# Final norm written in place, merge additions on GpSimd, and another slot for one table at the half change of an eight-core decoder kernel

## The chip, the cores and the metric

The kernel runs on the 8 cores of one Trainium2 chip, each core with its own sequence. The metric is the device time of the slowest core in microseconds (us). Before the change it was 3667.8 us, the median of 3 runs (3666.34 to 3668.78).

## The reference, cut to what matters

```python
for l in range(4):                       # per layer; 2048 positions, width 1024
    h = rmsnorm(x, norm1_g)
    zb, zc, zv, zu, ga, gs = split(h @ w_in)
    ya = zb * conv_causal(zc * zv)                 # short convolution branch
    ys = s5(zu)                                    # diagonal state space branch
    gy = gelu(ys); ys = gy * sigmoid(gy @ w_glu + b_glu)
    m  = sigmoid(ga) * (ya @ wb_conv) + sigmoid(gs) * (ys @ wb_ssm)   # merge
    x  = x + m @ w_out
    x  = x + (silu(gate) * up) @ w_down            # gate, up = rmsnorm(x) @ w_gate_up
return rmsnorm(x, final_g), ...                    # final norm, then states
```

## The kernel before

A core computes its sequence in two halves of 1024 positions: 4 layers of half 0, final norm and store, 4 layers of half 1, final norm and store. The **half change** is the passage from the end of half 0 into layer 0 of half 1. Half 0 has column blocks of 384, 384 and 272, half 1 has two of 512. The program records operations with their tiles, and then a list scheduler *inside the program* fixes each engine's order for good, with its own estimate of durations and of one DMA bus. So order is decided by a model and waits by the chip.

```python
def dma(self, eng, fn, r, w, nbytes, prio=None, extra=0.0):   # S.dma
    o.dur = 0.9 if eng == "pool" else 0.06     # the model's cost of an issue
    o.nbytes = nbytes; o.extra = extra
# ... in schedule():
    beg = max(bus, t + dur + 0.6)
    bus = beg + o.nbytes / self.DBW            # the model's one bus
    o.end = bus + 1.3 + o.extra

SP_ = Pool("sc", NSC - 4, lambda s: SC[:, s, :], reserve=2)    # five SC slots
TABP = Pool("tab", 2, ...)                                     # two table slots
TABC = Pool("tabc", 1, lambda s: R[:, 8:16, :]...)             # one more in R

def norm(half, blk, l, which, src=None):
    # ... squares on ACT, sum by ones-matmuls on PE, Ln and Exp on ACT into rs
    for kt in range(8):
        if which == "fg":                      # the final norm
            o = SP_.new()
            dve(scalar_tensor_tensor(out=o, in0=xi(), scalar=g, in1=rs, mult, mult))
            S.dma("sp", dma_start(out=yT[half, :, kt, ...], in_=o[:, 0:npr]), ...)
            if 8 in blk.ss:
                S.dma("sp", dma_start(out=ysT[:, kt, :], in_=o[:, npr:npr + NS]), ...)

def layer(half, l, after_blk, before_fd2=None):
    for f0 in range(2):                        # the state space input zu
        for mt in range(2):
            # PE: zu = w_in part of H; ACT: R[:, YS + f] = zu
            S.dma("sp", dma_start(out=du[f], in_=R[:, YS + f]))    # to DRAM ...
            S.dma("sp", dma_start(out=ut_, in_=du[f]))             # ... and back: UU
    def ssm_f(f):                              # one quarter of the state space branch
        alias = [("R", t, s) for t in range(8, 16) for s in range(9)] if f == 2 else []
        tab = (TABC if f == 2 else TABP).new()
        S.dma("sp", dma_start(out=tab[:, 0:TW], in_=stash[l, f]))  # its table
        # PE: state matmuls ps<-UU,TAB; DVE/ACT: scan, RBT, VT; PE: ps<-VT,TAB; ACT: gelu
        S.dma("sp", dma_start(out=dy[f], in_=yt))                  # to DRAM ...
        S.dma("sp", dma_start(out=R[:, YS + f], in_=dy[f]))        # ... and back
    # convolution: PE zc, zv, zb; ACT SC, DVE CIN; then GLU on R; then the merge:
                    dve(tensor_tensor(out=sg, in0=sg, in1=po, op=mult))
                    dve(tensor_tensor(out=R[:, MT[j]], in0=t_, in1=sg, op=add))

def unstage(where):     # half 1's x was loaded into idle tiles; ACT copies it into X
    for blk in BLKS[1]:
        for k in range(8):
            act(activation(out=X[:, k, ...], in_=t[...], func=AF.Copy))
```

(Arguments are shortened. A TensorE matmul of 128 x 128 by 128 x 512 is named by the tiles: `ps<-H,RING` multiplies the normed activation H by a weight slot, `ps<-R,RING` multiplies R.)

## Time and profile before

| | before |
|---|---|
| median of 3 runs, us | 3667.8 |
| profiled run: slowest core 1, us | 3684.6 |
| spans of its cores, us | 3655.5 to 3684.6 |
| PE busy | 3527.6 us, 96% |

The page's first part (busy us, share of the span, instructions of each engine) and the first group of its fifth part (busy time, mean ns of one, idle time just before and what ended it), kernel before:

```profile
PE 3527.6 (96%) x23912; PEld 1987.8 (54%) x23912; DVE 1699.6 (46%) x3049; ACT 1134.0 (31%) x2144; POOL 439.7 (12%) x639
...
L667 PE MATMUL ps<-H,RING 128*128 128x512 bf16 (+2 forms) x12160 | 2216.8, 343 | 22.5 <-DVE H L722 9.1
```

TensorE is the bound, and what this change can win is its pauses. Where it runs freely it is at its rate: one piece of the chain that ended last is 1008 matmuls of 512 columns in 217.60 us, 215.9 ns each. That agrees with the 215.7 ns that the Trainium skill gives for a warm N = 512 ("TensorE: Matmul & The Clock Gate", section "Wait — 56ns, not 53.3ns?").

The table by stretches around the half change, kernel before. Columns: stretch, its length, busy us (and instructions) of five engines, granted clock, DMA share, GB/s:

```profile
1896.00:1925.00 29.00, 25.02 (x149) 15.20 (x147) 23.41 (x43) 13.86 (x31) 2.11 (x4) 0.88 0.29 62
1925.00:2005.00 80.00, 59.41 (x653) 30.91 (x652) 38.54 (x71) 35.23 (x73) 3.17 (x6) 0.87 0.94 229
2005.00:2120.00 115.00, 114.85 (x533) 51.94 (x532) 54.65 (x82) 36.50 (x61) 7.91 (x15) 1.00 0.49 95
```

The first busy figure is PE: 3.98 + 20.59 us idle in the first two stretches. The waits of PE from 1890 to 2060 us (us in total, times, longest):

```profile
PE ps L1028 <- ACT X L1306: 10.0, 1, 10.0
PE ps L667 <- ACT CIN L1173: 5.6, 1, 5.6
PE ps L667 <- DVE X L1240: 4.0, 1, 4.0
PE ps L1102 <- DVE VT L1065: 2.9, 1, 2.9
```

They add up to 22.5 us. And the wait of DVE in the same passage that the change aims at:

```profile
DVE SC L712 <- DMA yT<-SC: 28.1, 8, 13.5
```

The final norm's writes need one of five SC slots, and a slot is free only when its store has landed. Timeline of SyncE's DMA issues (start, us, then what; the row's length runs from the first of its issues to the end of the last), kernel before:

```profile
1926.44 0.38 SPq L987 DMA_DIRECT2D du<-R  x1
...
1929.84 11.77 SPq L987 DMA_DIRECT2D du<-R  x3
1942.72 7.25 SPq L716 DMA_DIRECT2D yT<-SC  x4
1950.12 0.38 SPq L990 DMA_DIRECT2D UU<-du  x1
```

The first UU load leaves at 1950.12 us. Timeline of PE, with the idle time before a row and its releaser in brackets:

```profile
1923.67 20.88 PE L667 MATMUL ps<-H,RING 128*128 128x512 bf16 x96
1954.51 1.07 PE L1028 MATMUL ps<-UU,TAB 128*64 128x64 bf16 x32 [9.96 <-ACT X L1306]
...
1962.82 5.30 PE L667 MATMUL ps<-H,RING 128*128 128x512 bf16 x16 [5.65 <-ACT CIN L1173]
```

PE does 96 matmuls, stands for 10 us, and starts the first state matmul (`ps<-UU,TAB`) at 1954.51 us; the 16 after the next pause take 331 ns each (5.30 / 16) instead of 216. The DMA issues of 1896 to 2005 us (KB of one, median us from issue to landing):

```profile
yT<-SC SPq DMA_DIRECT2D x16, 192.0 KB, 4.2
...
du<-R SPq DMA_DIRECT2D x4, 256.0 KB, 18.3
```

### The profile page before, as it was taken

Reading aid. Unit: us, or ns where it says so; the run is one execution under the profiler, and the core shown is the slowest. Engines: PE = TensorE matmul, PEld = TensorE weight load, DVE = VectorE, ACT = ScalarE, POOL = GpSimd, SP = SyncE. Lnnn points to the kernel's source line nnn. Section 1 sums busy time; section 2 is a strip of 40 time slices with the busy share of each in tenths; the row PEclk is TensorE's granted clock in tenths of the full one; section 3 lists DMA queues with packets and bytes.
Section 4 is the critical chain, followed back from the end, with each engine's and each line's share of the span. In section 5 each row is a group of like instructions: output and inputs, shape, how many; then the busy total and the mean of one; then the engine's idle time right before and its main releaser. Section 6 shows DMA issues by size and latency. Waiting matters only on the chain.

```text
span 3684.6 us, 66888 instructions; the slowest of 8 cores (3655.5 to 3684.6 us)
## 1 busy us (share of the span) xinstructions
PE 3527.6 (96%) x23912; PEld 1987.8 (54%) x23912; DVE 1699.6 (46%) x3049; ACT 1134.0 (31%) x2144; POOL 439.7 (12%) x639
## 2 busy tenths in 40 slices
PE   6699999999999999999997999999999999999998
PEld 3466666666666666666653444444444444444443
DVE  8756455565545655543244532344224542255323
ACT  4442234432344323433034220332203421042202
POOL 4202210022100221000000000000000000000000
PEclk9799999999999999999998999989999999999999
DMA  7444567435564455854448444563445744474443
GB/s 159 112 80 70 113 148 144 81 70 113 145 141 86 70 113 139 185 109 75 75 83 217 77 80 70 109 144 60 79 80 106 159 69 81 69 146 79 79 70 86
DMA packets 252913, 384.11 MB, mean 104 GB/s; under 512 B 157744, under 2 KB 180912, under 8 KB 246960
## 3 DMA queue, kind: packets, MB, share of 16 engines
q0 software_dynamic: 67968, 243.30, 39.0%
q1 hardware_dynamic: 184624, 136.53, 12.6%
q8 instruction: 202, 3.31, 0.4%
q14 instruction: 119, 0.97, 0.1%
HBM read 567.06 MB, written 56.12 MB: 169 GB/s over the span
## 4 chain that ended last, share of the span: by engine, by line
PE 91%; DVE 3%; issue 3%; DMA 1%; ACT 1%; SPq 1%; DVEq 0%; ACTq 0%
PE ps L667 86%; PE ps L700 1%; PE ps L1102 1%; DMA yT<-SC 1%; DVE SC L559 1%; DVE H L722 1%; PE ps L904 1%; PE ps L1028 1%; PE ps L1075 0%; PE ps L891 0%; SPq L630 0%; DMA X<-xsT 0%; DVE X L1240 0%; DVE R L1220 0%; ACT H L698 0%
## 5 line engine op out<-in xcount | busy, mean ns | idle before, releaser
L667 PE MATMUL ps<-H,RING 128*128 128x512 bf16 (+2 forms) x12160 | 2216.8, 343 | 22.5 <-DVE H L722 9.1
L667 PEld LDWEIGHTS ps<-H,RING 128*128 128x128 bf16 x12160 | 1196.4, 99 | 980.1 <-issue 114.4
L667 PE MATMUL ps<-R,RING 128*128 128x384 bf16 (+2 forms) x6400 | 1164.8, 339 | 5.8 <-DVE X L1240 4.0
L667 PEld LDWEIGHTS ps<-R,RING 128*128 128x128 bf16 x6400 | 625.1, 98 | 505.9 <-issue 30.9
L1262 DVE TENSOR_TENSOR R<-SC,ps 128x384 bf16<-128x384 f32 (+2 forms) x440 | 255.7, 583 | 781.7 <-PE ps L667 763.8
L654 POOL DMA_DIRECT2D RING<-wpk x472 | 251.6, 534 | 2920.8 <-PE ps L667 2678.0
L1261 ACT ACTIVATE SC<-ps 128x384 f32<-128x384 f32 (+2 forms) x440 | 226.4, 515 | 1214.1 <-PE ps L667 1207.7
L1240 DVE TENSOR_TENSOR X<-X,ps 128x384 f32<-128x384 f32 (+2 forms) x480 | 270.8, 583 | 450.2 <-PE ps L667 447.1
L698 ACT ACTIVATE H<-X 128x384 bf16<-128x384 f32 (+2 forms) x304 | 156.5, 539 | 191.4 <-DVE X L1240 180.8
L722 DVE SCALAR_TENSOR_TENSOR H<-X,PRM,SC 128x384 bf16<-128x384 f32 (+2 forms) x304 | 190.9, 698 | 35.1 <-ACT SC L705 34.9
L1231 ACT ACTIVATE SC<-ps 128x384 f32<-128x384 f32 (+1 forms) x160 | 80.8, 515 | 265.5 <-PE ps L667 250.7
L1208 DVE TENSOR_TENSOR TB<-TB,ps 128x384 f32<-128x384 f32 (+2 forms) x160 | 90.4, 583 | 131.0 <-PE ps L667 114.0
L1232 DVE TENSOR_TENSOR SC<-SC,ps 128x384 f32<-128x384 f32 (+1 forms) x160 | 91.3, 582 | 87.8 <-PE ps L667 73.4
L1167 DVE TENSOR_TENSOR CIN<-ps,SC 128x384 f32<-128x384 f32 (+2 forms) x80 | 47.0, 587 | 182.7 <-ACT SC L1166 174.3
L559 DVE TENSOR_TENSOR SC<-TB 128x512 f32<-128x512 f32 (+1 forms) x160 | 120.0, 761 | 7.6 <-PE ps L904 0.6
L1153 ACT ACTIVATE TB<-ps 128x384 f32<-128x384 f32 (+1 forms) x160 | 79.6, 514 | 98.3 <-PE ps L667 97.8
L700 PE MATMUL ps<-H,ONESB 128*128 128x384 bf16 (+2 forms) x320 | 77.6, 349 | 25.1 <-ACT H L698 25.1
L1235 DVE TENSOR_TENSOR R<-TB,SC 128x384 bf16<-128x384 f32 (+1 forms) x160 | 91.6, 587 | 10.4 <-DVE SC L1232 0.9
L559 POOL TENSOR_TENSOR TB<-TB 128x512 f32<-128x512 f32 (+1 forms) x72 | 89.2, 1242 | 53.6 <-ACT H L698 32.5
L1220 DVE TENSOR_TENSOR R<-R,SC 128x384 bf16<-128x384 bf16 (+2 forms) x80 | 46.6, 588 | 74.5 <-ACT SC L1218 73.0
L895 ACT ACTIVATE TAB<-ps 128x512 bf16<-128x512 f32 x60 | 35.5, 597 | 132.0 <-PE ps L891 131.8
L1166 ACT ACTIVATE SC<-ps 128x384 f32<-128x384 f32 (+2 forms) x80 | 41.0, 514 | 95.5 <-PE ps L667 95.4
(179 smaller groups left out, 1621.2 us busy)
## 6 DMA issues: line engine op xcount, KB each, us to landing
RING<-wpk POOLq DMA_DIRECT2D x440, 512.0 KB, 7.0
TAB<-stash SPq DMA_DIRECT2D x21, 1792.0 KB, 9.4
stash<-TAB SPq DMA_DIRECT2D x15, 1792.0 KB, 7.8
R<-stash SPq DMA_DIRECT2D x7, 1792.0 KB, 14.3
RING<-wpk POOLq DMA_DIRECT2D x32, 384.0 KB, 5.9
du<-R SPq DMA_DIRECT2D x32, 256.0 KB, 9.3
UU<-du SPq DMA_DIRECT2D x32, 256.0 KB, 6.5
dy<-YY SPq DMA_DIRECT2D x32, 256.0 KB, 6.4
```

Of the source, the lines that this page charges most:

```text
L559: fn = lambda e: e.tensor_tensor(out=out(), in0=a(), in1=b(), op=op)
L654: S.dma("pool", lambda e: e.dma_start(out=t[:, 0:n], in_=wpk[l, ui, :, 0:n]), [("X",) + gate] if gate else (), [(t,)], 128 * n * 4, prio=- ...
L667: subs.append((lambda e, u=u, kw=kw, c=c, src=src, i=i: e.matmul(ps[:, 0:blk.n], lhsT=u.ap(kw, c), rhs=src(blk), start=(i == 0), stop=(i = ...
L698: act(lambda e, kt=kt: e.activation(out=hq(kt), in_=xin(kt)[0], func=AF.Square), xin(kt)[1], qkeys(kt, blk), n)
L700: S.pe([(lambda e, kt=kt: e.matmul(ps[:, 0:n], lhsT=ONESB[:], rhs=hq(kt), start=(kt == 0), stop=(kt == 7)), qkeys(kt, blk) + [C_("ONESB")] ...
L722: dve(lambda e, kt=kt, xi=xi, g=g: e.scalar_tensor_tensor(out=H[:, kt, blk.c0:blk.c0 + n], in0=xi(), scalar=g, in1=rs[:, 0:n], op0=ALU.mul ...
L1208: dve(lambda e, po=po, n=n, t_=t_, blk=blk: e.tensor_tensor(out=t_[:, blk.c0:blk.c0 + n], in0=t_[:, blk.c0:blk.c0 + n], in1=po[:, 0:n], op ...
L1232: dve(lambda e, sg=sg, po=po, n=n: e.tensor_tensor(out=sg[:, 0:n], in0=sg[:, 0:n], in1=po[:, 0:n], op=ALU.mult), [(sg,), (po,)], [(sg,)], n)
L1235: dve(lambda e, sg=sg, n=n, t_=t_, blk=blk, j=j: e.tensor_tensor(out=R[:, MT[j], blk.c0:blk.c0 + n], in0=t_[:, blk.c0:blk.c0 + n], in1=sg[ ...
L1240: dve(lambda e: e.tensor_tensor(out=X[:, j, blk.c0:blk.c0 + n], in0=X[:, j, blk.c0:blk.c0 + n], in1=ps[:, 0:n], op=ALU.add), [(ps,)] + xke ...
L1261: act(lambda e, sg=sg, pg=pg, n=n: e.activation(out=sg[:, 0:n], in_=pg[:, 0:n], func=AF.Silu), [(pg,)], [(sg,)], n, tset="silu")
L1262: dve(lambda e, sg=sg, pu=pu, n=n, blk=blk, ti=ti: e.tensor_tensor(out=R[:, ti, blk.c0:blk.c0 + n], in0=sg[:, 0:n], in1=pu[:, 0:n], op=ALU ...
```

## The change

Three things. (1) The final norm writes its result into X itself and the stores read X, so no SC slot is needed. (2) The 160 merge additions go from VectorE to GpSimd. (3) At the half change the second table (f = 1) takes the idle activation slots R 8 to 15, and the third goes where the second was. The aim is to free the half change from the slots, and VectorE from some work. Two smaller edits come with (1): in half 0 the norm's writes rank 40 operations later in the scheduler's order of preference (`FO`), and the eight small ysT stores become one.

```diff
+FO = 40
+MENG = "pool"
...
             if which == "fg":
                 g = PRM[:, PFG + kt:PFG + kt + 1]
-                o = SP_.new()
-                dve(lambda e, kt=kt, xi=xi, g=g, o=o: e.scalar_tensor_tensor(
-                    out=o[:, 0:n], in0=xi(), scalar=g, in1=rs[:, 0:n], op0=ALU.mult, op1=ALU.mult),
-                    xik + [(rs,), pk], [(o,)], n, dur=STT_(n))
                 npr = blk.np
-                S.dma("sp", lambda e, kt=kt, o=o: e.dma_start(out=yT[half, :, kt, blk.c0:blk.c0 + npr], in_=o[:, 0:npr]),
-                      [(o,)], [], 128 * npr * 4)
-                if 8 in blk.ss:
-                    S.dma("sp", lambda e, kt=kt, o=o: e.dma_start(out=ysT[:, kt, :], in_=o[:, npr:npr + NS]), [(o,)], [], 8192)
+                dve(lambda e, xi=xi, g=g: e.scalar_tensor_tensor(
+                    out=xi(), in0=xi(), scalar=g, in1=rs[:, 0:n], op0=ALU.mult, op1=ALU.mult),
+                    xik + [(rs,), pk], xik, n, dur=STT_(n), prio=len(S.ops) + (FO if half == 0 else 0))
+                S.dma("sp", lambda e, kt=kt: e.dma_start(out=yT[half, :, kt, blk.c0:blk.c0 + npr], in_=X[:, kt, blk.c0:blk.c0 + npr]),
+                      [k_ for k_ in xik if k_[2] != 8], [], 128 * npr * 4)
+        if which == "fg" and 8 in blk.ss:
+            S.dma("sp", lambda e: e.dma_start(out=ysT, in_=X[:, :, 1024:1040]), [("X", k, 8) for k in range(8)], [], 65536)
...
-                alias = [("R", t, s) for t in range(8, 16) for s in range(9)] if f == 2 else []
-                tab = (TABC if f == 2 else TABP).new()
+                cf = 1 if half == 1 and l == 0 else 2
+                alias = [("R", t, s) for t in range(8, 16) for s in range(9)] if f == cf else []
+                tab = (TABC if f == cf else TABP).new()
...
-                    dve(lambda e, sg=sg, n=n, t_=t_, blk=blk, j=j: e.tensor_tensor(out=R[:, MT[j], ...], in0=t_[...],
-                        in1=sg[:, 0:n], op=ALU.add), [(sg,), (t_, blk.i)], rkeys(MT[j], blk), n)
+                    S.op(MENG, lambda e, sg=sg, n=n, t_=t_, blk=blk, j=j: e.tensor_tensor(out=R[:, MT[j], ...], in0=t_[...],
+                        in1=sg[:, 0:n], op=ALU.add), [(sg,), (t_, blk.i)], rkeys(MT[j], blk),
+                        TT_(n) if MENG == "dve" else 0.2 + 2.3e-3 * n)
```

More of the change, by code (lines that the diff above doesn't have):

```diff
@@ L710, in norm @@
                 g = PRM[:, PFG + kt:PFG + kt + 1]
-                o = SP_.new()
-                dve(lambda e, kt=kt, xi=xi, g=g, o=o: e.scalar_tensor_tensor(
-                    out=o[:, 0:n], in0=xi(), scalar=g, in1=rs[:, 0:n], op0=ALU.mult, op1=ALU.mult),
-                    xik + [(rs,), pk], [(o,)], n, dur=STT_(n))
                 npr = blk.np
-                S.dma("sp", lambda e, kt=kt, o=o: e.dma_start(out=yT[half, :, kt, blk.c0:blk.c0 + npr], in_=o[:, 0:npr]),
-                      [(o,)], [], 128 * npr * 4)
-                if 8 in blk.ss:
-                    S.dma("sp", lambda e, kt=kt, o=o: e.dma_start(out=ysT[:, kt, :], in_=o[:, npr:npr + NS]), [(o,)], [], 8192)
-            else:
+                dve(lambda e, xi=xi, g=g: e.scalar_tensor_tensor(
[5 more added lines that the diff above has]
+            S.dma("sp", lambda e: e.dma_start(out=ysT, in_=X[:, :, 1024:1040]), [("X", k, 8) for k in range(8)], [], 65536)
+        if which != "fg":
+            for kt in range(8):
+                xi = lambda kt=kt: xin(kt)[0]
+                xik = xin(kt)[1]
                 g = pcol(l, which, kt)
@@ L1234, in layer @@
                     t_ = tj[jj]
-                    dve(lambda e, sg=sg, n=n, t_=t_, blk=blk, j=j: e.tensor_tensor(out=R[:, MT[j], blk.c0:blk.c0 + n], in0=t_[:, blk.c0:blk.c0 + n],
-                                                                                in1=sg[:, 0:n], op=ALU.add), [(sg,), (t_, blk.i)], rkeys(MT[j], blk), n)
+                    S.op(MENG, lambda e, sg=sg, n=n, t_=t_, blk=blk, j=j: e.tensor_tensor(out=R[:, MT[j], blk.c0:blk.c0 + n], in0=t_[:, blk.c0:blk.c0 + n],
+                                                                                in1=sg[:, 0:n], op=ALU.add), [(sg,), (t_, blk.i)], rkeys(MT[j], blk),
+                         TT_(n) if MENG == "dve" else 0.2 + 2.3e-3 * n)
         def xadd(ps, j, blk):
```

## The prediction

> **What bounds it now.** TensorE. The page's first part has PE busy 3527.6 of 3684.6 us (96%); the chain that ended last is 91% PE. DVE (46%), ACT (31%) and POOL (12%) have room. In the table by stretches PE idles about 62 us of the first 150 us (start-up, untouched), 41 us of 150 to 1592 us, 25 us of the half change (1896 to 2005 us), 16 us of 2005 to 3640 us and 14 us of the tail. Only half change and tail are touched strongly.
>
> **Half change, before.** In the timeline DVE's final-norm writes go to five SC slots, each held until its store has landed: DVE waits 28.1 us for yT stores, up to 13.5 us at once. SP issues in order, so the UU<-du loads stand behind stores that wait for those writes; the first leaves at 1950.1 us and lands about 3.8 us later. The first state matmul starts at 1954.5 us, after 10.0 us of PE idle. The view names ACT's X copy as releaser; I read the UU load as the true one. ACT is held by X copies that wait for the final norm: 5.6 us of wait for CIN. With 4.0 us (x additions behind norms on DVE) and 2.9 us (VT) PE loses 22.5 us, plus some 6 us of matmuls at half rate after pauses (16 of 128x512 took 333 ns each instead of 215).
>
> **What the change does there.** The 24 writes go into X and need no slot, so stores leave once the norm is done, the first into a time without DMA traffic (about 1898 to 1912 us). SP is no longer blocked by them; UU comes earlier. The second table's load moves from 1963.9 us to about 1921 us; the third takes the later place. New: copies into X wait for stores to land (median 4.2 us), in order on ACT. I expect 12 to 20 of the 28 us back: the round trip over du (18.3 us to landing) stays, and the same passage in a later layer still idles 4 to 5 us in 200.
>
> **Merge.** 160 additions leave DVE (43.6 + 34.8 + 14.1 = 92.5 us). POOL needs 1.31 us for a 128x512 addition where DVE needs 0.69; estimated from that, 64 of 1.35, 64 of 1.05 and 32 of 0.75 us make 178 us. One merge group takes PE 12 x 215 ns = 2.6 us, so POOL keeps up. DVE isn't the limit there: gain 0 to 4 us. The danger is POOL's order: an addition behind a weight load that waits for a ring slot, or the reverse. The Trainium skill, "SBUF — State Buffer", section "Who interferes with whom", says that a DVE instruction with two SBUF inputs contends with a GpSimd instruction that reads SBUF; the DVE products here read one operand from PSUM, so only GLU, convolution and norms can collide. This trace has norm writes of up to 1617 ns against a median of 617.
>
> **Tail.** Store waits of 0.68, 0.29 and 0.89 us go: 1 to 2 us.
>
> **Sum.** 15 + 2 + 1 = 18 us: 3650 us, range 3634 to 3667. Faster by over 2%: 1%; within 2%: 96%; slower: 3%.
>
> **What would show it.** PE idle from 1896 to 2005 us falls from 25 to about 10 us; the first UU load leaves before 1946 us; DVE never waits for yT stores; DVE busy falls by about 92 us, POOL's rises by about 180; waits for POOL's merge results stay below 3 us.
>
> **What would make it wrong.** The instruction order comes from a scheduler's model inside the program; a new order may open waits elsewhere. ACT may stall on copies that wait for stores. Weight loads may slip behind additions.

## More of the kernel before

In one run of the kernel before, one die ran at a clock of 0.83 and took 4227 to 4233 us, the other at 0.98 and took 3660 to 3666. Executions in which one die ran at a lower clock are left out of the means. *Median of undisturbed cores*: over all runs of a kernel in one job, the median span of those cores whose mean granted clock was at least 0.9795. It is compared only with the kernel before in the same job, and it has no interval of its own: taken run by run, it moves by 3 to 6 us between runs of the kernel before inside one job, so a difference of 1 to 2 us is no more than a hint. Where a range stands beside it ("resampled"), that is an estimate, from drawing the recorded runs anew with repetition.

## The result, and the profile after

After: 3664.11 us, median of 4 runs (3662.38 to 3670.76); before, in the same rounds, 3668.06 us. The ratio is 0.9993, 95% interval 0.9976 to 1.0011. A ratio is the mean time of one kernel's fast runs over that of the other's of the same rounds, so it is not quite the ratio of the two medians. The predicted gain of 18 us (ratio 0.995) lies outside the interval.

The page, kernel after:

```profile
PE 3504.0 (96%) x23912; PEld 1979.7 (54%) x23912; DVE 1618.6 (44%) x2889; ACT 1141.7 (31%) x2151; POOL 608.7 (17%) x799
...
L669 PE MATMUL ps<-R,RING 128*128 128x384 bf16 (+2 forms) x6400 | 1162.1, 339 | 19.7 <-DMA R<-dy 11.4
...
L1240 POOL TENSOR_TENSOR R<-TB,SC 128x384 bf16<-128x384 f32 (+1 forms) x160 | 168.1, 1063 | 113.1 <-DVE SC L1237 101.4
```

The work moved as intended: DVE 1699.6 to 1618.6 us, POOL 439.7 to 608.7. (PE's busy sums are not comparable: the profiled core before ran at a mean clock of 0.973, the one after at 0.981.) But a wait that was not there appears, for `R<-dy`. The same stretches, kernel after:

```profile
1896.00:1925.00 29.00, 25.02 (x150) 15.25 (x149) 26.98 (x51) 13.90 (x33) 2.11 (x4) 0.88 0.32 71
1925.00:2005.00 80.00, 73.27 (x472) 34.09 (x469) 32.60 (x53) 35.98 (x72) 5.28 (x10) 0.96 0.89 193
2005.00:2120.00 115.00, 100.70 (x709) 47.27 (x710) 44.39 (x77) 35.27 (x61) 25.75 (x27) 0.94 0.55 117
```

From 1896 to 2005 us PE idles 3.98 + 6.73 = 10.7 us instead of 24.6, as predicted. The next stretch gives it back: PE busy falls from 114.85 to 100.70 us. Over all three it is 199.28 before and 198.99 after. The lower clock moved along: 0.87 then 1.00 before, 0.96 then 0.94 after. PE's waits, 1890 to 2060 us, kernel after:

```profile
PE ps L669 <- DMA R<-dy: 11.4, 3, 8.9
PE ps L669 <- ACT TB L1158: 5.5, 1, 5.5
PE ps L669 <- DVE X L1246: 4.0, 1, 4.0
PE ps L1107 <- DVE VT L1070: 1.8, 2, 0.9
```

With 0.4 us for GLU's result they sum to 23.1 us, against 22.5 before. (The 5.5 us stand behind ACT's copies into X, which now wait 15.7 us for stores to land.) On all eight cores `R<-dy` costs 11.4 to 14.6 us; before, no core has this wait. DVE's waits for stores are gone. SyncE's issues, kernel after:

```profile
1925.61 0.38 SPq L991 DMA_DIRECT2D du<-R  x1
1926.13 21.54 SPq L717 DMA_DIRECT2D yT<-X  x7
1947.83 0.38 SPq L991 DMA_DIRECT2D du<-R  x1
1948.36 3.87 SPq L717 DMA_DIRECT2D yT<-X  x5
...
1955.12 14.74 SPq L991 DMA_DIRECT2D du<-R  x2
1969.96 1.10 SPq L994 DMA_DIRECT2D UU<-du  x1
```

Seven stores keep SyncE for 21.54 us; a single issue, which takes some 0.33 us in quiet times, took up to 8.3 us for a store and 13.9 us for a `du`. (Before, single issues were long too: a `dy<-YY` of this passage took 9.1 us.) `UU<-du` leaves at 1969.96 us, 20 us *later* than before, where I had expected it earlier. PE's timeline, kernel after:

```profile
1924.68 45.06 PE L669 MATMUL ps<-H,RING 128*128 128x512 bf16 x208
1975.24 12.24 PE L669 MATMUL ps<-H,RING 128*128 128x512 bf16 x48 [5.50 <-ACT TB L1158]
1987.64 0.70 PE L1033 MATMUL ps<-UU,TAB 128*64 128x64 bf16 x32
...
2043.63 0.58 PE L669 MATMUL ps<-R,RING 128*128 128x512 bf16 x1 [8.89 <-DMA R<-dy]
2045.72 9.38 PE L669 MATMUL ps<-R,RING 128*128 128x512 bf16 x32 [1.51 <-DMA R<-dy]
```

PE now does 256 matmuls (208 + 48) ahead of the first state matmul instead of 96. These are convolution and gate work that depends on nothing in the state space branch. At the other end, from 2033 us, only GLU is left, which needs all of `R<-dy`, and PE stands; the matmuls after that pause take 293 ns each (9.38 / 32). The chain that ended last says the same (start, us, what):

```profile
1922.20 27.80 DMA yT<-X
1950.56 21.30 DMA yT<-X
...
2030.66 12.21 DMA dy<-YY
2042.93 2.66 DMA R<-dy
```

And the DMA issues, which landed far later for the stores:

```profile
yT<-X SPq DMA_DIRECT2D x16, 192.0 KB, 16.6
...
du<-R SPq DMA_DIRECT2D x4, 256.0 KB, 17.2
```

To measure stages on every core I used the ones-matmuls of the norms as marks and took medians over cores (six of the eight have all marks: some matmul records are missing). "Passage" runs from the last ones-matmul of half 0's final norm to the first of the second norm in half 1's layer 0. One profile each, us:

| segment | before | after | merge additions alone | change without them |
|---|---|---|---|---|
| half 0: FFN part of layers 0, 1, 2 | 282.1, 281.6, 282.0 | 282.9, 283.1, 283.8 | 283.0, 283.2, 283.7 | 281.5, 281.1, 281.9 |
| half 0: merge part of layers 1, 2 | 179.4, 181.4 | 177.6, 176.8 | 178.9, 177.9 | 178.4, 181.3 |
| passage | 193.2 | 190.1 | 194.0 | 187.9 |
| half 1: merge part of layers 1, 2, 3 | 179.4, 174.2, 174.4 | 176.0, 178.1, 174.2 | 176.5, 179.3, 174.2 | 178.6, 174.2, 174.4 |
| tail (from the last mark) | 11.6 | 10.6 | 11.6 | 10.2 |

The passage won 3.1 us, not 15. It also spread: 192.8 to 194.5 us over the cores before, 185.0 to 196.2 after, and the slowest core is the metric. What splits the cores is a wait, and it shows what sets the start of the state branch. On cores 1, 5 and 6 (185.0 to 187.8 us) PE reaches its first state matmul without a pause, each time 55.7 us after the passage's first mark, though UU was issued at 42.5, 30.0 and 40.1 us: there it was PE's order, with its 256 matmuls, that made the state branch late, and not the late UU. On cores 0, 3 and 7 (192.4 to 196.2 us) PE waits 4.3 to 6.6 us more, behind ACT's copies.

### The profile page after: what moved, and what is told of

It is laid out like the page before. It is cut to its first block, busy times and chain, and to the rows that moved or that the text cites. A ratio compares the mean times of both kernels' runs of the same rounds, so it can differ in the third digit from the quotient of the medians.

```text
span 3663.7 us, 67385 instructions; the slowest of 8 cores (3647.5 to 3663.7 us)
## 1 busy us (share of the span) xinstructions
PE 3504.0 (96%) x23912; PEld 1979.7 (54%) x23912; DVE 1618.6 (44%) x2889; ACT 1141.7 (31%) x2151; POOL 608.7 (17%) x799
## 4 chain that ended last, share of the span: by engine, by line
PE 88%; DVE 4%; issue 3%; DMA 3%; ACT 1%; SPq 1%; DVEq 0%; ACTq 0%; POOL 0%; POOLq 0%
PE ps L669 83%; DMA yT<-X 1%; PE ps L702 1%; PE ps L1107 1%; DVE SC L561 1%; DVE H L726 1%; PE ps L1033 1%; PE ps L908 1%; PE ps L1080 0%; DVE X L1246 0%; DMA scv<-CIN 0%; SPq L632 0%; PE ps L895 0%; DMA X<-xsT 0%; DVE R L1225 0%
## 5 line engine op out<-in xcount | busy, mean ns | idle before, releaser
L669 PE MATMUL ps<-R,RING 128*128 128x384 bf16 (+2 forms) x6400 | 1162.1, 339 | 19.7 <-DMA R<-dy 11.4
L726 DVE SCALAR_TENSOR_TENSOR H<-X,PRM,SC 128x384 bf16<-128x384 f32 (+2 forms) x304 | 183.0, 672 | 35.0 <-ACT SC L707 34.8
L1240 POOL TENSOR_TENSOR R<-TB,SC 128x384 bf16<-128x384 f32 (+1 forms) x160 | 168.1, 1063 | 113.1 <-DVE SC L1237 101.4
L561 DVE TENSOR_TENSOR SC<-TB 128x512 f32<-128x512 f32 (+1 forms) x160 | 124.1, 785 | 8.1 <-PE ps L908 0.6
L561 POOL TENSOR_TENSOR TB<-TB 128x512 f32<-128x512 f32 (+1 forms) x72 | 89.3, 1242 | 42.3 <-DVE R L835 20.7
## 6 DMA issues: line engine op xcount, KB each, us to landing
R<-stash SPq DMA_DIRECT2D x7, 1792.0 KB, 14.8
```

Source lines behind the costliest of these rows:

```text
L561: fn = lambda e: e.tensor_tensor(out=out(), in0=a(), in1=b(), op=op)
L669: subs.append((lambda e, u=u, kw=kw, c=c, src=src, i=i: e.matmul(ps[:, 0:blk.n], lhsT=u.ap(kw, c), rhs=src(blk), start=(i == 0), stop=(i = ...
L726: dve(lambda e, kt=kt, xi=xi, g=g: e.scalar_tensor_tensor(out=H[:, kt, blk.c0:blk.c0 + n], in0=xi(), scalar=g, in1=rs[:, 0:n], op0=ALU.mul ...
L1240: S.op(MENG, lambda e, sg=sg, n=n, t_=t_, blk=blk, j=j: e.tensor_tensor(out=R[:, MT[j], blk.c0:blk.c0 + n], in0=t_[:, blk.c0:blk.c0 + n], ...
```

## The experiments

All were timed in 5 rounds, in three jobs of four. The kernel before had undisturbed cores of 3658.2, 3658.6 and 3660.7 us in jobs 1, 2 and 3. My first theory, Q: the stores fill SyncE's queue, so the input of the state space branch comes late. Its rival: the stores' transfers themselves take the DMA engines and delay all other data. Later came M, the *moved wait*: the round trip zu, du, UU, state matmuls, dy, R, GLU has a length of its own, and only a fixed stock of other matmuls can run beside it; where PE eats that stock decides where it idles, not whether. In the quoted expectations Q and M are these two; B and D are rivals that blame the data traffic, and A is one that blames ACT's copies into X.

| label | what | ratio of fast runs [95%] | undisturbed cores against before | passage |
|---|---|---|---|---|
| e_merge | before + additions on GpSimd | 1.0006 [0.9993, 1.0020] | +2.0 | 194.0 |
| e_nomerge | change without them | 0.9989 [0.9976, 1.0003] | -7.1 | 187.9 |
| e_poolst | half-0 stores issued by GpSimd | 1.0001 [0.9986, 1.0017] | -1.0 | 189.4 |
| e_nostore | 3 of 24 half-0 stores | 0.9992 [0.9979, 1.0006] | -4.5 | 188.0 |
| x_nb0 | e_nomerge, another order | 0.9997 [0.9952, 1.0042] | -7.2 | 194.1 |
| x_poolnb0 | both of these, no additions moved | 0.9989 [0.9950, 1.0028] | -9.1 | 187.0 |
| x_late_uu | most stores after the UU loads | 0.9985 [0.9937, 1.0032] | -10.5 | 184.5 |
| e_table | before + table placement | 0.9981 [0.9941, 1.0021] | -2.4 | 192.4 |
| e_again | the change, unedited | 1.0006 [0.9992, 1.0019] | -1.4 | 189.4 |
| e_inplace | before + in-place norm only | 0.9990 [0.9975, 1.0005] | -5.3 | 187.8 |
| e_late | the change + late stores | two fast runs, no ratio | -6.9 | 184.8 |
| x_best1 | x_late_uu + X copies on GpSimd | 0.9987 [0.9972, 1.0002] | -6.6 | 188.4 |

All results were correct but that of e_nostore. The order of events in the passage, us after its first mark, medians of cores; then how many matmuls PE's order has between that mark and the first state matmul, and what PE idles in the passage (pauses of over 0.15 us):

| kernel | first UU issued | first state matmul | last state-branch matmul ends | last `R<-dy` issued | matmuls ahead | PE idle, us |
|---|---|---|---|---|---|---|
| before | 26.0 | 30.4 | 80.8 | 94.3 | 96 | 18.5 |
| e_table | 25.8 | 30.4 | 73.1 | 93.9 | 96 | 17.7 |
| e_inplace | 36.8 | 55.7 | 97.3 | 113.4 | 256 | 16.2 |
| after | 43.3 | 59.1 | 101.1 | 115.5 | 256 | 17.5 |
| e_again | 42.1 | 57.1 | 99.5 | 115.4 | 256 | 17.3 |
| e_nomerge | 40.7 | 56.2 | 98.9 | 114.0 | 256 | 16.7 |
| e_poolst | 13.1 | 54.8 | 96.1 | 114.3 | 200 | 15.9 |
| e_nostore | 27.0 | 52.2 | 90.8 | 112.0 | 240 | 12.5 |
| x_nb0 | 29.9 | 41.2 | 90.4 | 102.4 | 136 | 18.8 |
| x_poolnb0 | 10.8 | 30.3 | 89.6 | 108.6 | 96 | 13.8 |
| x_late_uu | 23.2 | 40.1 | 87.1 | 106.0 | 184 | 11.6 |
| e_late | 24.5 | 40.1 | 87.2 | 109.0 | 184 | 12.0 |
| x_best1 | 24.0 | 40.1 | 88.4 | 111.5 | 184 | 14.8 |

### e_merge: the additions alone

```diff
 # before, and:
-  dve(lambda e, ...: e.tensor_tensor(out=R[:, MT[j], ...], ..., op=ALU.add), ...)
+  S.op("pool", lambda e, ...: e.tensor_tensor(out=R[:, MT[j], ...], ..., op=ALU.add), ...)
```

> The kernel before with only the merge additions moved to GpSimd. If the merge is worth 0 to 4 us as predicted, the time is 0 to 4 us under before and the half change passage (from the last norm matmul ahead of the half change to the first of the next norm, 193.2 us median of cores in the profile of before) stays within 1 us. The segments of half 0 with a merge (181.4 us in layer 2) should fall by 2 to 4 us and those with the FFN (282.0 us) rise by about 1 us, if the small differences between the two profiles come from the merge. Rival: those come from the new instruction order as a whole; then they stay at the values of before.

Measured: 1.0006 [0.9993, 1.0020], cores +2.0 us (resampled +0.8 to +4.1), passage 194.0 against 193.2, within the expected 1 us. The additions alone do not gain; if anything they cost. By the segments they win in two merge parts (-3.5 us in half 0 layer 2, -2.9 us in half 1 layer 1), lose about 5 us in another (half 1 layer 2) and 1 to 2 us in each of three FFN parts, where no addition runs.

### e_nomerge: the change without the additions

```diff
-MENG = "pool"
+MENG = "dve"
```

> The changed kernel with the merge additions back on VectorE: in-place norm and the new table place alone. If the parts are independent, the half change passage is about 190 us as in the changed kernel (before: 193.2) and the time about 2 to 4 us under before; the half 0 segments go back to those of before (181.4 and 282.0 us). Rival: the additions on GpSimd cost something at the half change; then the passage is clearly under 190 us.

Measured: 0.9989 [0.9976, 1.0003], cores -7.1 us, passage 187.9. So the other two parts are worth about 4 us (by the fast runs) to 7 us (by the cores), more than the expected 2 to 4, and PE still waits 12.5 us for `R<-dy`, 11.2 at once. The additions are not the source of the moved wait.

### e_poolst: the half-0 stores issued by GpSimd

```diff
-S.dma("sp", ... out=yT[half, ...], in_=X[...])
+S.dma("pool" if half == 0 else "sp", ... out=yT[half, ...], in_=X[...])
```

> The changed kernel with the 24 stores of the final norm of half 0 issued by GpSimd instead of SyncE. Theory Q (the stores fill SyncE's queue, its issues block for up to 13.9 us, and du and UU stand behind them): no SyncE issue in the half change takes over 5 us, the first UU load leaves before 1950 us instead of 1970, the wait of TensorE for R from dy (11.4 us) goes, and the passage falls from 190 to about 178 to 182 us; the time falls by 8 to 12 us. Rival B (the DMA engines are 99% busy from 1914 to 1970 us, so order does not matter): UU still leaves after 1960 us and the passage stays within 2 us of 190. Rival A (ScalarE's copies into X, which wait for the stores, are what holds): R from dy comes earlier but TensorE's wait for the sigmoid into TB (5.5 us) grows by as much.

Measured: 1.0001, cores -1.0 us, passage 189.4. No store of yT in half 0 is left on SyncE, and the first UU load leaves 30 us earlier than in the changed kernel (13.1 instead of 43.3 us after the mark). SyncE's timeline and PE's waits, e_poolst:

```profile
1937.95 0.41 SPq L994 DMA_DIRECT2D UU<-du  x1
...
2010.27 14.15 SPq L1123 DMA_DIRECT2D R<-dy  x1
```

```profile
PE ps L669 <- DMA R<-dy: 10.0, 2, 8.6
PE ps L669 <- DMA RING<-wpk: 9.1, 1, 9.1
```

Yet the first state matmul starts at 54.8 us. The edit also changed PE's order, but 200 matmuls still stand ahead of it, and PE waits 7.1 to 9.6 us among them for weight loads (`RING<-wpk`), which GpSimd issues and which now come late. The wait for `R<-dy` is still there. Theory Q alone falls; its forecast that no SyncE issue takes over 5 us failed too, since a single `R<-dy` took 14.15 us. Rival A does not show either: no wait for TB is left.

### e_nostore: 3 of 24 stores of half 0 (result wrong)

```diff
+                if half == 1 or kt == 0:
                   S.dma("sp", ... out=yT[half, ...], in_=X[...])
```

> Wrong on purpose: of half 0's final norm only one of eight row tiles is stored (3 of 24 stores). It shows what the stores cost in all. Theory Q and rival B both expect the passage to fall from 190 to about 176 us, that of an ordinary layer (179.4 and 174.2 us), and the time by about 14 us; if it stays above 185 us, stores are not the cause and the round trip over du or the staging is.

Measured: 0.9992, cores -4.5 us, passage 188.0; the first output is not a number. Nearly all store traffic is gone, PE's order is close to that of the changed kernel (240 matmuls ahead of the state branch), and PE still waits for `R<-dy`, 8.3 us on the profiled core and 5.6 or more on the others. The rival that blames the transfers needed a passage below 185 us and falls as the main cause; Q had expected the same and falls with it. Nor are the stores needed for long issues on SyncE: here one `R<-dy` took 14.3 us and one `UU<-du` 11.0.

### x_nb0: the same work in another order

```diff
 # e_nomerge, and the scheduler's estimate is told that these stores move nothing:
-                      [k_ for k_ in xik if k_[2] != 8], [], 128 * npr * 4)
+                      [k_ for k_ in xik if k_[2] != 8], [], 128 * npr * 4 if half == 1 else 0)
```

> The changed kernel with the additions on VectorE, and the program's scheduler told that half 0's 24 final stores move no bytes; the work is the same, only the order changes, so that the state matmuls stand earlier in TensorE's order. Theory M (moved wait): the stretch is a chain zu, du, UU, state matmuls, dy, R beside a fixed stock of convolution and gate matmuls that fills TensorE's time. The change let TensorE use up the stock first and started the chain 33 us later (first state matmul at 1987.6 instead of 1954.5 us), so the idle time came back as the wait for R from dy. Then with the chain earlier that wait falls from 12.5 to under 4 us and the half change passage from 187.9 to 178 to 183 us, unless the real UU load (behind 24 stores) lands too late, in which case the idle time shows before the first state matmul. Rival D (the wait for R from dy is set by slow transfers at the end of the chain, whatever its start): the wait stays above 8 us.

Measured: 0.9997, passage 194.1 (cores 186.8 to 199.3). The instructions are those of e_nomerge and only their order differs: 136 matmuls instead of 256 stand ahead of the state matmuls. Since the edit changes nothing but the bytes that the scheduler's model books on its bus, it was these bytes that made the model put the state branch late. PE's waits, x_nb0:

```profile
PE ps L669 <- ACT SC L1171: 12.4, 1, 12.4
PE ps L1107 <- issue: 6.3, 1, 6.3
...
PE ps L1033 <- issue: 3.5, 1, 3.5
```

The wait for `R<-dy` is gone on every core and the idle time is back ahead of the first state matmul, 12.4 us in one piece, with 9.8 us more between the state matmuls. The expectation had named this outcome as the exception to its 178 to 183 us. This is what M says: one order pays at the end, the other at the front. What holds the front is ACT: its copies into X overwrite what the stores still read, and ACT's waits, x_nb0, show it:

```profile
ACT X L1312 <- DMA yT<-X: 15.4, 5, 14.2
```

PE's 12.4 us are for a convolution result that ACT writes only after these copies; the first UU load, too, leaves only at 1954.15 us on this core, behind seven stores that kept SyncE for 17.51 us. Order alone gains nothing over e_nomerge (cores -7.2 and -7.1 us) as long as the stores hold up SyncE and ACT. That the passage is 6 us longer I would not build on: the profiled run was the slowest of the five with enough undisturbed cores (their median 3656.2 us, in the others 3647.0 to 3655.3).

### x_poolnb0: the order of x_nb0 and the stores on GpSimd

```diff
-S.dma("sp", ...)
+S.dma("pool" if half == 0 else "sp", ..., 128 * npr * 4 if half == 1 else 0)
```

> As x_nb0, and the 24 stores are issued by GpSimd, so that SyncE's queue holds only the chain. Theory M: first state matmul before 1960 us, no wait for R from dy over 4 us, passage 176 to 182 us, time 6 to 12 us under the changed kernel without the moved additions. Rival D: the wait for R from dy stays above 8 us. Rival B (the DMA engines are full in the stretch): the first UU load still lands after 1965 us and the passage stays near 188.

Measured: 0.9989, cores -9.1, passage 187.0: the expected 176 to 182 was missed. The order is again another one (96 matmuls ahead). The state matmuls start at 30.3 us and `R<-dy` costs nothing, but PE waits 5.2 to 7.8 us for weights, whose loads GpSimd issues beside the stores, and 3 to 5 us for UU. A third place for the wait.

### x_late_uu: most stores behind the UU loads

```diff
 # e_nomerge, and blocks 1 and 2 (16 of 24 stores, and ysT) are kept back:
+                if half == 0 and blk.i >= 1:
+                    held.append(st_)
+                else:
+                    st_([])
 # in layer(), after the zu part:
+        if half == 1 and l == 0:
+            for st_ in held:
+                st_([(zus[1], 0)])        # not before the second UU load has landed
+            unstage(staged[0])            # and the copies into X after them
```

> The changed kernel with the additions on VectorE; the stores of column blocks 1 and 2 (16 of 24) and the copies into X wait until the second UU load has landed. The chain gets the DMA queues first. Theory M: the first state matmul comes before 1955 us and the wait for R from dy falls under 6 us, but the copies out of TB come late, so TensorE waits for the sigmoid into TB or for convolution tiles; the passage is 180 to 188 us. If only the late start of the chain counted it would be about 178.

Measured: 0.9985 [0.9937, 1.0032], cores -10.5 us (resampled -11.2 to -10.0), the best, passage 184.5 on the median and 183.9 to 184.8 over the cores. Both conditions are met here: the stores hold up neither SyncE nor ACT before the first state matmul (UU leaves at 23.2 us), and PE's order has that matmul at 40.1. (That is 1966.8 us on the profiled core, not before 1955 as expected: the edit gave PE another order too, with 184 matmuls ahead of it. All eight cores reach it at 40.1, without waiting for UU.) PE's waits, x_late_uu:

```profile
PE ps L669 <- ACT RL L1081: 5.6, 1, 5.6
PE ps L669 <- DVE X L1254: 4.0, 1, 4.0
PE ps L1115 <- DVE VT L1078: 2.9, 1, 2.9
PE ps L1088 <- ACT YY L1122: 2.2, 1, 2.2
```

With two short ones they sum to 15.8 us, against 22.5 before and 23.1 after. The 5.6 us stand where the 16 copies into X run as one block on ACT.

### e_table: the table placement alone

```diff
 # before, and:
+                cf = 1 if half == 1 and l == 0 else 2
-                tab = (TABC if f == 2 else TABP).new()
+                tab = (TABC if f == cf else TABP).new()
```

> The kernel before with only the new place of the second table. Theory M: the first state matmul stays near 1954 us and the second comes soon after (before: 1975, behind a table load issued at 1963.9 us); since TensorE's idle time lies ahead of the first one and the chain's end has slack in the kernel before, the passage changes by less than 3 us from 193.2. If the table were what held the stretch, the passage would fall by 8 us or more.

Measured: 0.9981 [0.9941, 1.0021], cores -2.4, passage 192.4 (193.2). The state branch ends 7.7 us sooner (73.1 against 80.8), but the last `R<-dy` leaves only 0.4 us sooner: a small effect, as expected, and no moved wait.

### e_again: the changed kernel once more

> The changed kernel itself once more, unaltered, to have its cores beside those of its parts on one chip. By the sum of the parts measured so far on undisturbed cores (in-place norm with new table place 7.0 us under before, additions on GpSimd 2.0 us over it) its cores should lie 3 to 6 us under before; if they lie 7 us or more under, the additions cost nothing inside the changed kernel.

Measured: 1.0006 [0.9992, 1.0019], cores -1.4 us (resampled -5.0 to +2.3); the expected 3 to 6 us was missed. The passage is 189.4, and `R<-dy` costs PE 17.7 us on the profiled core. It is the changed kernel's second measurement and agrees with the first: no gain that the noise lets one see.

### e_inplace: the in-place norm alone

```diff
 # the changed kernel, with
-MENG = "pool"
+MENG = "dve"
-                cf = 1 if half == 1 and l == 0 else 2
+                cf = 2
```

> The kernel before with only the final norm in place. If the parts add up, its undisturbed cores lie 4 to 5 us under before (7.0 with the new table place, 2.4 from the table alone) and the passage is 188 to 190 us. Theory M: the first state matmul comes over 50 us after the last final-norm matmul, as in the changed kernel, so the moved wait comes from the stores in place and not from the table; rival: it stays near 30 us as before and the table is what moved it.

Measured: 0.9990, cores -5.3 us (resampled -7.7 to -2.0), just past the expected 4 to 5, and 3.8 us below e_again in the same job; passage 187.8 (expected 188 to 190). The first state matmul starts at 55.7 us (before: 30.4), and `R<-dy` costs 13.0 to 14.3 us on the four undisturbed cores. So the in-place norm, with the two smaller edits that belong to it, makes the moved wait by itself, and most of the gain. (Over the three undisturbed cores that have all marks, the first state matmul is also at 55.7 and the passage at 187.0.)

### e_late: the changed kernel with late stores

The edit of x_late_uu on the changed kernel, with the additions on GpSimd.

> The changed kernel, additions on GpSimd included, with the 16 stores of column blocks 1 and 2 and the copies into X held until the second UU load has landed. Theory M: the wait of TensorE for R from dy (11.4 us) goes and the passage falls from 190.1 to 184 to 187 us, as it did with the additions on VectorE (187.9 to 184.5). If the additions on GpSimd interact with the chain, it stays above 188.

Measured: only two of its runs were fast (3665.51 and 3659.73 us), so there is no ratio; cores -6.9 us, passage 184.8, at most 1.0 us of wait for `R<-dy`. The late stores help in the same place with the additions on GpSimd; the gain on the cores is 3.6 us less than x_late_uu's in another job, about what the additions cost elsewhere.

### x_best1: x_late_uu and the X copies on GpSimd

```diff
-                act(lambda e, ...: e.activation(out=X[...], in_=t[...], func=AF.Copy), ...)
+                pool(lambda e, ...: e.tensor_copy(X[...], t[...]), ...)
```

> As x_late_uu (additions on VectorE, stores held), with the 16 copies into X on GpSimd instead of ScalarE, where they ran as one block of 10 us and TensorE waited 5.7 us behind them. If that wait is only ScalarE's order, it goes, and the passage falls from 184.5 to 178 to 181 us. Against it: a new instruction order may open another wait, and 16 copies on GpSimd delay weight loads; then the passage stays at 183 us or more.

Measured: 0.9987, cores -6.6 us, passage 188.4 (expected 178 to 181). The 5.6 us behind the copies went away and this came back (PE's waits, x_best1):

```profile
PE ps L669 <- DMA R<-dy: 7.7, 1, 7.7
```

On six of the eight cores it is 5.7 to 8.6 us. The last `R<-dy` left at 111.5 us instead of 106.0. Removing one more wait again moved it.

## Why the prediction was right or wrong

The time, 3664.11 us, lies in the range (3634 to 3667) only because that range reached up to almost no gain; the forecast gain of 18 us did not come. Point by point:

- **What bounds it:** right. PE is 96% busy before and after.
- **DVE's wait for stores (28.1 us) goes:** right; no such wait is left.
- **PE idle from 1896 to 2005 us falls from 25 to about 10 us:** right, 10.7 us. But this was the wrong place to stop reading. "I expect 12 to 20 of the 28 us back" is **the step that failed**. It took the idle time before the first state matmul for removable. The passage won 3.1 us (3.8 in e_again), because 11 to 18 us came back as a wait for `R<-dy`, some 90 us after the old pause. PE's listed waits sum to 22.5 us before and 23.1 after. I had named the danger ("a new order may open waits elsewhere") and given it no weight in the sum.
- **"SP is no longer blocked by them; UU comes earlier" (leaving before 1946 us):** wrong, 1969.96 us. The five slots had also been a brake: with them the norm's writes went on until 1961.5 us, and 13 of the 24 stores left ahead of the first UU load. Without them the writes end at 1929.9 us, all 24 stores leave ahead of UU, and one issue held SyncE for up to 8.3 us with the `du` issues behind it. In e_poolst, where the stores leave SyncE, UU goes 30 us earlier, and in e_nostore 16. That is why I read SyncE's queue as the reason for the late UU; what makes one issue last 13.9 us no run isolates, and issues as long occur without the stores (e_nostore). The late UU was not what cost the time: with this order PE comes to it only at 55.7 us.
- **The order of PE:** not in my sum at all. The change puts 256 instead of 96 matmuls ahead of the state matmuls. Nearly this order without the stores (e_nostore, 240 ahead) gives 188.0, and early UU with 200 ahead (e_poolst) 189.4, with a wait for weights of its own. The early order with the stores still ahead of UU and of ACT's copies (x_nb0) has no wait for `R<-dy`, but pays at the front and gains nothing either. The stores out of the way and the state matmuls earlier (x_late_uu, e_late) give 184.5 and 184.8. So it is shown that PE's order makes the wait for `R<-dy` and that the in-place norm makes the order. That both order and stores must go for a gain is shown less cleanly, because each edit also made the scheduler choose another order. x_poolnb0 had both too, but PE waited for weights, 187.0.
- **The round trip sets the end:** the estimate saw the trip over `du` (18.3 us) only as something that stays. The whole chain from zu to GLU is what matters: its start moved from 30.4 to 59.1 us after the mark and its last `R<-dy` from 94.3 to 115.5. M as I first put it is too strong, though: PE's idle time in the passage is 18.5 us before and 17.5 after, but 11.6 in x_late_uu, so order does decide in part whether PE idles. What sets the trip's own length stays open: on the profiled core the last `R<-dy` but one took 12.0 us from issue to landing and the last 2.7, with a table load of 1792 KB issued 2 us before the slow one, and no run moves that load.
- **"ACT may stall on copies that wait for stores":** right as a warning, and again without weight in the sum. ACT waits 15.7 us for them on the profiled core of the changed kernel, and PE 5.5 us behind ACT; on cores 1, 5 and 6 PE does not wait there.
- **Merge, "gain 0 to 4 us":** wrong, and by the cores wrong in sign. POOL's time was well estimated (178 us; measured 168.1), DVE's busy time fell by 81.0 us (92 forecast), and PE never waited for POOL's results (ACT and DVE did, 18 times each, 18.7 and 26.2 us in all, at most 2.6 at once). But the additions cost 2.0 us alone and 3.8 us inside the changed kernel (e_again against e_inplace, which differs by the table too; resampled -0.6 to +7.7). Against e_nomerge the changed kernel loses 5.3 us in the three FFN parts, where no addition runs, and 2.2 in the passage, and wins 4.2 in the merge parts. So the reordering is the likely way; one sign is that ACT loads its function tables 125 times against 118 before, with 124 in e_merge and 119 in e_nomerge. This stays open: no run isolates it. GpSimd also keeps an SC slot longer than DVE did, which no run isolates either.
- **Port contention:** the danger that I cited from the Trainium skill ("SBUF — State Buffer", section "Who interferes with whom") was hardly put to the test. The DVE product over SC and PSUM took 686 ns (128x512) before and 688 after, and on the profiled core of the changed kernel no norm write, no convolution product and only 3 of the 80 GLU products overlap one of the moved additions (436 ns in the middle for these 3, 443 for the rest of their size). The contention itself is in both traces, as the page has it: in the changed kernel 121 norm writes of 128x384 take 603 to 620 ns, and the 7 that overlap another elementwise instruction of GpSimd (L561, a helper's line, in half 0) up to 1619, 1419 in the middle; before, the 7 of this kind also take 1419 in the middle.
- **Tail, 1 to 2 us:** right, 11.6 to 10.6 us.
- **Table:** predicted without a number of its own; -2.4 us on the cores alone.

The sum as it came: half change -3 to -4, tail -1, merge +2 to +4, together about 0 to -3 us; e_again's cores show -1.4. The best version, x_late_uu, is 10.5 us or 0.3% under the kernel before on undisturbed cores, about half of what I had expected, and by fast runs alone still "same".

## What to carry to other kernels

An idle gap in front of a long dependent chain is only worth what is left after the chain's end is looked at too: ask which independent work the engine will use to fill the gap, and what it will then lack when the chain's result is due. A buffer limit that makes an engine wait may also pace a queue, so before it is lifted, ask what stands behind the flood, and let the transfers that feed the critical chain go first. When an order is fixed by a model inside the program, every edit also changes the order, so test the order by itself.

## What the Trainium skill lacked or had wrong

- "DMA: Bandwidth & Descriptors", section "Issuing engines are not separate DMA queues", says that several issuing engines only save the time on the sequencer, "which is usually small relative to the DMA itself". Here one SyncE issue took 0.33 us in quiet times but up to 8.3 us for a 192 KB store and 13.9 us for a `du` transfer while much was outstanding, and with the stores on GpSimd the UU load left 30 us earlier (13.1 against 43.3 us). The page has no figure for an issue under load. That all issuers share the same engines would fit the 9.1 us wait for weights with the stores on GpSimd, but the weight loads also stand in GpSimd's own order with these stores, so the run does not tell the two apart.
- "GPSIMD Engine Reference", section "3.1 Elementwise — side-by-side cycle accounting", gives GpSimd's addition as 1.96 times slower than VectorE's, for 2048 fp32 elements. Nothing wrong there: on 128x512 with a bf16 result, a case that the section lacks, it was 1.83 times (1265 against 691 ns).
- No page warns that moving 160 such additions off a VectorE that is 46% busy can fail to gain (+2.0 us alone on undisturbed cores). The way is not isolated; the new order is the likely one.
